# Seven products over all feature tiles in a network's second half, and a quarter of a modulation's dots moved into an earlier stage

## The chip, the core and the metric

The kernel runs on one core of one Trainium2 chip. The metric is the device time of one execution in microseconds (us), the median of several runs. Engines are named as the profile names them: TensorE (PE, with its weight loads PEld), VectorE (DVE), ScalarE (ACT), GpSimd (POOL) and SyncE (SP, which only issues DMAs here).

## The reference

A trunk of two layers runs on 640 tokens at once (128 context tokens, 512 latent ones; 1024 features, so 8 feature tiles of 128). Layer 0 mixes tokens by a two-way SSD scan, layer 1 by differential attention. Behind each mixer stands a gated network, which is where most of the change lies:

```python
def conv_ffn(h, up_w, conv_w, conv_b, down_w):
    u = dwconv(h @ up_w, conv_w, conv_b)      # 1024 -> 2 x 2816, width 3 along the tokens
    a, v = jnp.split(u, 2, axis=-1)
    return (jax.nn.silu(a) * v) @ down_w      # 2816 -> 1024
```

Each sub-layer is normalised, modulated by shift, scale and gate, and added to the residual. The modulation of a layer is `silu(c) @ mod_w + mod_b`, 6 x 1024 values for each of two conditioning vectors (context, latent). Layer 1's ("the second modulation") is first needed by the norm in front of the attention.

## The kernel before

Activations lie feature-major, as tiles of 128 features by 640 tokens. Every large product is made of float32 values split in a high and a low half ("h" and "l", whi and wlo): high x high, high x low and low x high, three matmuls for one. Weights come by DMA as `raw` units of up to 128 x 1024, listed in order by `weight_units`. `cast` makes the halves: ScalarE copies the high one, VectorE subtracts for the low one. For units in the set `summed` the low half is made without VectorE: ScalarE writes the negative of the high half, and a DMA that GpSimd issues adds the weights from DRAM to it (line 181). Before, `summed` holds only up-projection weights of layer 1.

**The network** (`ffn`) computes 22 pairs of hidden tiles (a, v). The plain form takes, for each of the two tiles, 8 feature tiles x 3 products x 2 column halves (256 and 384 columns). From pair `S0[l]` on it uses a scheme with seven block products instead of eight: feature tiles are taken in two groups of `ns`, tokens in two halves of 320, and sums of weight blocks and of activation halves (T1 to T4) are multiplied. `pair8` does so in layer 1 with ns = 4, all eight feature tiles, from pair 4 on. `pair7` does so in layer 0 with ns = 2, on four of the eight feature tiles (the other four stay plain), from pair 16 on. `operands` builds the T tiles (VectorE adds and subtractions, ScalarE copies); in layer 0 they lie in the buffers of the modulation's rows. `epilogue` does convolution, silu and product and splits the result into mh and ml. In layer 1 ml too is made by ScalarE and an accumulating DMA.

The pairs are worked in blocks (`SUB`): after each block, one pair ahead, `project_out` multiplies it with the down weights for all 8 output tiles and `gate_add` adds to the residual `xr`. Layer 0 has three blocks, layer 1 five. `project_last` does the last block and starts the next norm (`norm_task`, by token halves A and B); `start_tiles` begins the next product with three output tiles, half A first.

**The second modulation** is computed by VectorE: `mod_rows` on TensorE serves layer 0 only, and `mod_rest` (line 598) loads the 48 rows of 512 KB of layer 1 one at a time into two `mw` buffers and takes two dots a row (line 620). It is a background task: `hook` is called after every few matmuls (six, most often) and lets tasks emit a next piece, each with its own pace. In layer 0 this task is drained before the down-projection of the second block.

The order of each engine's instructions is set when the program is built, by a list scheduler which takes what is ready, the earlier written first. Engines then run in that order. A pool of SBUF tiles that opens on the room of an earlier one waits until all of that one's tiles are released.

Stages in the trace: scan until 422 us, its output projection (`po`) 422 to 559, layer 0's start tiles (`st`) 559 to 582, its network until 1025, attention until 1390, layer 1's network until the end.

Of the kernel before, what the change touches and what calls it, by code (L numbers as in the profile page):

```python
# [18 lines left out]
P = 128  # L19
# [17 lines left out]
SUB = ((0, 8), (8, 15), (15, 22)), ((0, 4), (4, 8), (8, 12), (12, 16), (16, 22))  # L37
MIDS = 9, 6
# [3 lines left out]
NS = 2, 4  # L42
S0 = 16, 4
# [6 lines left out]
class Step:  # L50


    def __init__(self, ctx, tc, a):
        self.ctx, self.tc, self.nc, self.a = ctx, tc, tc.nc, a
        self.tasks = []
        self.ticks = 0
        self.wi = 0
        self.normt = {}
        self.ready = []
        self.px = None  # L60
        self.modtask = None
        self.late = []
        self.down = False
# [265 lines left out]
    def project_last(self, h, ks, g, nextnorm, ks_last=None, parts="AB"):  # L329
# [268 lines left out]
    def mod_rest(self, l, t0, pool):  # L598
# [3 lines left out]
        cb = pool.tile([P, 2, D], F32, tag="cbc", name="cbc", bufs=1)  # L602
        nc.sync.dma_start(cb, a["cbc"])
        for c in range(2):
            sb = self.pw.tile([P, 1024], F32, tag="raw", name="csil", bufs=RAW)
            self.act(sb, cb[:, c, :], AF.Tanh, scale=0.5)
            self.stt(cb[:, c, :], sb, 1.0, cb[:, c, :], ALU.add, ALU.mult)
            nc.vector.tensor_scalar(cb[:, c, :], cb[:, c, :], 0.5, None, ALU.mult)
        yield 4
        for t in range(t0 - 1, 48):  # L610
            if t < 47:
                nxt = pool.tile([P, 1024], F32, tag="mw", name="mw", bufs=2)
# [6 lines left out]
            for c in range(2):  # L619
                nc.vector.tensor_tensor_reduce(w if c else junk, w, cb[:, c, :], 1.0, 0.0, ALU.mult, ALU.add,  # L620
                                               self.mod[l][:, t, c:c + 1])
                yield 2 if self.down else 7
# [17 lines left out]
    def ffn(self, l, h, nextnorm, pool):  # L640
# [16 lines left out]
        def epilogue(p, ua, uv):  # L657
# [6 lines left out]
            hi = self.slot("mh", f"mh{p}", F32R, bufs=MIDS[l], pool=pool)  # L664
            lo = self.slot("ml", f"ml{p}", F32R, bufs=MIDS[l], pool=pool)
            self.act(hi, cv, AF.Copy)
            if l and p < FT - 1:
# [17 lines left out]
        ns = NS[l]  # L685
        cut = lambda t, j: t[:, j * TH:(j + 1) * TH]

        def operands(out):
# [4 lines left out]
            for i in range(ns):  # L693
# [10 lines left out]
                if l:  # L704
                    hi, lo = (pool.tile([P, 3 * TH], F32R, tag=f"T{nm}{i}", name=f"T{nm}{i}", bufs=1) for nm in "hl")
                    x4 = tuple(cut(t, 1) for t in h[i])
                    late.append((x4, cut(t43, 0)))
                    parts = (slice(0, T), t12), (slice(T, T + TH), cut(t43, 1))
                else:
                    if i:  # L710
                        both = pool.tile([P, 2, 3 * TH], F32R, tag="cbc", name=f"T{i}", bufs=1)
                        hi, lo = both[:, 0, :], both[:, 1, :]
                    else:
                        hi, lo = (pool.tile([P, 3 * TH], F32R, tag="mw", name=f"T{nm}{i}", bufs=2) for nm in "hl")
                    t4 = self.slot("f", f"T4_{i}", F32R, bufs=NF)
                    x4 = cut(t4, 0), cut(t4, 1)
                    late.append((x4, cut(t43, 0)))
                    parts = (slice(0, T), t12), (slice(T, T + TH), cut(t43, 1))
# [63 lines left out]
        def pair7(p, B, Ts, rest, _):  # L782


            (B11, _), (B21, B22) = B
            T1, T2, T3, T4 = Ts
            u = self.wi
            self.wi += 3
            self.prefetch(u + 6)
            self.cast(u + 2)  # L790
            wa, ws, wv = (self.wcast[u + j] for j in range(3))
            w, r0 = ns * P, 2 * ns * P
            ua, uv = (self.slot("f", "uraw", bufs=NF) for _ in range(2))
            p5 = self.slot("f", "p5", bufs=NF)[:, :TH]
            ps = self.dense_ps("up")
            X, Y = ps[:, :TH], ps[:, 512:512 + TH]
            block(X, wa, 0, B11, True, True)
            with self.tc.high_priority():
                self.act(ua[:, lft], X, AF.Copy)
            block(Y, wa, w, B21, True, False)  # L800
            ps = self.dense_ps("up")
            V, Z = ps[:, :TH], ps[:, 512:512 + TH]
            block(V, ws, 0, T1, True, True)
            with self.tc.high_priority():
                self.act(p5, V, AF.Copy)
            block(X, ws, w, T2, False, True, True)
            with self.tc.high_priority():
                self.tt(ua[:, rgt], X, p5, ALU.add)
            block(Y, wa, r0, rest[0], False, True)
            self.tt(ua[:, lft], Y, ua[:, lft], ALU.add)  # L810
            block(Z, ws, 3 * w, B22, True, False)
            self.cast(u + 3)
            block(Z, wa, r0, rest[1], False, True)
            self.tt(ua[:, rgt], Z, ua[:, rgt], ALU.add)
            block(X, ws, 2 * w, T3, False, True, True)
            with self.tc.high_priority():
                self.act(uv[:, rgt], X, AF.Copy)
            self.cast(u + 4)
            block(V, wv, r0, rest[1], False, True, True)
            self.tt(uv[:, rgt], V, uv[:, rgt], ALU.add)  # L820
            block(X, wv, w, T4, False, True, True)
            block(X, wv, r0, rest[0], False, True, True)
            with self.tc.high_priority():
                self.act(uv[:, lft], X, AF.Copy)
            epilogue(p, ua, uv)

# [5 lines left out]
        def pair(p, more):  # L832
            if p >= S0[l]:
# [3 lines left out]
                return pair8(p, more) if l else pair7(p, *sevens)  # L837
# [5 lines left out]
        self.deep = 2 if l else 1  # L843
        sevens = []
        self.began = None
        self.seven = self.add(operands(sevens), 1) if l else None
        for s, (k0, k1) in enumerate(SUB[l]):
            self.down = False
            while done < min(k1 + 1, FT):
                pair(done, done + 1 < min(k1 + 1, FT))  # L850
                done += 1
            self.down = True
            if s == 1 and not l:
                self.drain(self.modtask)
                self.seven = self.add(operands(sevens), 4)
            if s == len(SUB[l]) - 1 and self.modtask:
                self.drain(self.modtask)
            if s < len(SUB[l]) - 1:
                self.project_out(mid, range(k0, k1), self.gate(l, 1))
            else:  # L860
                self.project_last(mid, range(k0, k1), self.gate(l, 1), nextnorm, parts="CD" if l else "AB")
# [269 lines left out]
    def ssd(self, h, dtps, nextnorm, pool):  # L1131
# [51 lines left out]
        for i in range(KT):  # L1183
            xi = self.slot("f", f"xr{i}", bufs=NF)
            self.nc.sync.dma_start(xi, self.a["xT"][i])
            self.x.append(xi)
        self.project_out(hy, range(8), self.gate(0, 0))
# [3 lines left out]
        self.modtask = self.add(self.mod_rows(2, pool, 7))  # L1191
        self.project_last(hy, range(8), self.gate(0, 0), nextnorm)

# [238 lines left out]
    def weight_units(self):  # L1432
# [9 lines left out]
        def ffn(l):  # L1442
            done = 0
            out = []
            ns = NS[l]
            m = ns * 4 * P // 1024
            for k0, k1 in SUB[l]:
                while done < min(k1 + 1, FT):
                    seven = done >= S0[l]
                    pl = ("x", "w") if seven and l else (None, None)  # L1450
# [19 lines left out]
    def run(self):  # L1470
        tc, nc, a = self.tc, self.nc, self.a
        self.units = self.weight_units()
        last = [u for u, x in enumerate(self.units) if x[0] is not None and x[0].name == a["w_up"].name][-2 * FT:]
        after = [u for u in last if self.units[u - 1][0] is not None and self.units[u - 1][0].name != a["w_up"].name]
        self.summed = set(last[5:]) - set(after)
# [10 lines left out]
        with tc.tile_pool(name="psd", bufs=3, space=PSUM) as self.psd:  # L1486
            self.stages(tc, hs, norm)
        with (tc.tile_pool(name="psb", bufs=6, space=PSUM, reuse_waits="tile") as self.psb,
              tc.tile_pool(name="ffn1", bufs=1) as pool):
            self.px = pool  # L1490
            self.modtask = None
            self.ffn(1, hs[3], self.final_task, pool)
            for t in reversed(list(self.tasks)):
                self.drain(t)

    def stages(self, tc, hs, norm):

        with tc.tile_pool(name="sconst", bufs=1) as cp:
# [6 lines left out]
        with tc.tile_pool(name="ffn0", bufs=1) as pool:  # L1505
            self.px = pool
            mw = lambda: pool.tile([P, 1024], F32, tag="mw", name="ntm", bufs=2)

# [105 lines left out]
```

## Time and profile before

| | us |
|---|---|
| median of 3 runs | 1846.98 |
| lowest, highest | 1846.07, 1847.43 |
| the profiled execution | 1847.95 |
| its span, first to last instruction | 1846.2 |
| PE busy in the span | 1802.7 |
| DVE busy | 1490.5 |
| ACT busy | 1038.7 |

The granted TensorE clock is 0.994 of full speed. Durations of matmuls overlap, since they are pipelined: the time of a stage is read from where it starts and ends, and divided by the number of matmuls. A group's line gives the engine, the operation, output and inputs by name, the shape and the count, then busy us, mean ns of one, and the idle time in front with what ended it. VectorE's and ScalarE's instructions overlap by some 0.07 us, so the distance of two starts is a little less than a duration.

### The profile page before, as it was taken

What the parts mean: (1) busy time and instruction counts of PE and PEld (TensorE: products, weight loads), DVE (VectorE), ACT (ScalarE), POOL (GpSimd) and SP (SyncE); (2) the same over time, 40 slices, a digit from 0 to 9 for tenths busy, and PEclk for the clock granted to TensorE, in tenths of its full rate; (3) what the DMA queues carried; (4) which work ended last, traced back from release to release, by engine and by line L of the source; (5) the groups of instructions that cost most, each with busy time, mean ns of one, the idle gap of its engine ahead of it and who ended that gap; (6) DMA issues with size and microseconds to landing.
All of it is one profiled execution on the core that took longest, in us unless ns stands there. A gap on an engine that the chain in (4) does not pass through costs nothing.

```text
span 1846.2 us, 33204 instructions
## 1 busy us (share of the span) xinstructions
PE 1802.7 (98%) x13070; PEld 1704.8 (92%) x13070; DVE 1490.5 (81%) x2969; ACT 1038.7 (56%) x1987; POOL 49.2 (3%) x60
## 2 busy tenths in 40 slices
PE   7999999999999999999999999999999999999997
PEld 5899999999989999999999988888899999999996
DVE  5689999999748999987585878777878877768784
ACT  3489686879326441343353556656636554746561
POOL 0000000000000000000000000000000010101110
PEclk9999999999999999999999999999999999999998
DMA  9844343445533556542122211211124445546451
GB/s 337 264 135 138 99 148 105 121 137 179 187 133 104 194 183 214 194 133 78 57 82 91 80 48 60 65 55 38 55 83 110 104 114 141 126 129 154 122 137 58
DMA packets 90051, 230.28 MB, mean 125 GB/s; under 512 B 10428, under 2 KB 17192, under 8 KB 89768
## 3 DMA queue, kind: packets, MB, share of 16 engines
q1 hardware_dynamic: 81256, 207.13, 34.8%
q0 software_dynamic: 8064, 20.52, 6.6%
q8 instruction: 102, 1.67, 0.4%
q10 hardware_dynamic: 576, 0.52, 0.1%
q14 instruction: 53, 0.43, 0.1%
HBM read 215.29 MB, written 5.96 MB: 120 GB/s over the span
## 4 chain that ended last, share of the span: by engine, by line
PE 86%; DVE 6%; ACT 3%; DMA 3%; issue 2%; SPq 0%; POOL 0%; DVEq 0%; POOLq 0%; ACTq 0%
PE up L110 27%; PE po L110 25%; PE z L110 6%; PE x L110 5%; PE st L110 5%; PE yp L110 3%; PE bc L110 3%; PE q L110 2%; PE k L110 1%; PE modrow L110 1%; PE sl L110 1%; ACT whi L101 1%; PE ov L110 1%; PE v L110 1%; ACT e L101 1%
## 5 line engine op out<-in xcount | busy, mean ns | idle before, releaser
L101 ACT ACTIVATE whi<-raw 128x1024 fp32r<-128x1024 f32 (+3 forms) x243 | 227.8, 939 | 277.3 <-PE po L110 167.4
L107 DVE TENSOR_TENSOR wlo<-raw,whi 128x1024 fp32r<-128x1024 f32 (+3 forms) x207 | 227.0, 1097 | 43.0 <-ACT whi L101 37.5
L104 DVE SCALAR_TENSOR_TENSOR xr<-po,mod,xr 128x256 f32<-128x256 f32 (+2 forms) x279 | 107.8, 432 | 108.9 <-PE po L110 108.8
L110 PE MATMUL po<-mh,whi 128*128 128x256 f32 (+1 forms) x704 | 166.9, 310 | 0.0
L110 PE MATMUL po<-ml,whi 128*128 128x256 f32 (+1 forms) x704 | 166.6, 309 | 0.0
L110 PE MATMUL po<-mh,wlo 128*128 128x256 f32 (+1 forms) x704 | 166.3, 309 | 0.0
L110 PE MATMUL up<-h01l,whi 128*128 128x256 f32 (+1 forms) x596 | 146.2, 308 | 0.0
L110 PE MATMUL up<-h01h,whi 128*128 128x256 f32 (+1 forms) x596 | 146.1, 310 | 0.1
L110 PE MATMUL up<-h01h,wlo 128*128 128x256 f32 (+1 forms) x596 | 145.6, 308 | 0.0
L110 PEld LDWEIGHTS po<-mh,whi 128*128 128x128 f32 x704 | 128.0, 188 | 0.7 <-ACT mh L101 0.5
L110 PEld LDWEIGHTS po<-ml,whi 128*128 128x128 f32 x704 | 128.2, 188 | 0.2 <-DVE ml L107 0.2
L110 PEld LDWEIGHTS po<-mh,wlo 128*128 128x128 f32 x704 | 128.2, 188 | 0.0
L110 PEld LDWEIGHTS up<-h01h,whi 128*128 128x128 f32 x596 | 108.9, 188 | 1.5 <-ACT uraw L101 1.1
L110 PEld LDWEIGHTS up<-h01l,whi 128*128 128x128 f32 x596 | 109.1, 188 | 0.0
L110 PEld LDWEIGHTS up<-h01h,wlo 128*128 128x128 f32 x596 | 109.0, 188 | 0.0
L110 PE MATMUL up<-h11h,whi 128*128 128x320 f32 (+1 forms) x368 | 107.3, 309 | 0.0
L110 PE MATMUL up<-h11l,whi 128*128 128x320 f32 (+1 forms) x368 | 107.2, 309 | 0.0
L110 PE MATMUL up<-h11h,wlo 128*128 128x320 f32 (+1 forms) x368 | 107.1, 309 | 0.0
L104 DVE SCALAR_TENSOR_TENSOR cv<-uraw,fcw,cv 128x511 f32<-128x511 f32 (+1 forms) x176 | 85.3, 545 | 14.8 <-ACT cv L101 14.8
L104 DVE SCALAR_TENSOR_TENSOR ca<-uraw,fcw,ca 128x127 f32<-128x127 f32 (+1 forms) x176 | 86.7, 545 | 8.8 <-ACT ca L101 7.5
L101 ACT ACTIVATE mh<-cv 128x640 fp32r<-128x640 f32 x44 | 32.5, 738 | 88.8 <-DVE cv L107 88.8
L101 ACT ACTIVATE whi<-s 128x512 fp32r<-128x512 f32 (+1 forms) x96 | 52.8, 571 | 52.2 <-DVE s L107 22.7
(531 smaller groups left out, 5074.4 us busy)
## 6 DMA issues: line engine op xcount, KB each, us to landing
raw<-in_w_up SPq DMA_DIRECT2D x88, 512.0 KB, 3.4
mw<-in_modT SPq DMA_DIRECT2D x48, 512.0 KB, 3.8
raw<-in_w_in SPq DMA_DIRECT2D x40, 512.0 KB, 5.5
rb<-rowd SPq DMA_DIRECT2D x40, 512.0 KB, 5.4
raw<-in_w_qkv SPq DMA_DIRECT2D x24, 512.0 KB, 3.3
mr<-in_mod SPq DMA_DIRECT2D x44, 256.0 KB, 5.2
wlo<-in_w_up POOLq DMA_DIRECT2D x17, 512.0 KB, 5.2
mp<-in_modp SPq DMA_DIRECT2D x32, 256.0 KB, 5.4
```

Of the source, the lines that this page charges most:

```text
L101: return self.nc.scalar.activation(out, in_, func, **k)
L104: return self.nc.vector.scalar_tensor_tensor(out, in0, s, in1, op0, op1)
L107: return self.nc.vector.tensor_tensor(out, a, b, op)
L110: return self.nc.tensor.matmul(out, lhsT, rhs, start=start, stop=stop, skip_group_check=more)
```

## The change

- Layer 0's network uses the form of layer 1 (`pair8`, ns = 4) from pair 10 on; `pair7` goes. It has layer 1's five blocks, and 6 buffers of mh and ml instead of 9. The T tiles get a pool of their own (`sums`), which in layer 0 opens before pair 8, on the room of the modulation's rows: the row task is drained there, and the pool of its rows closed. The operands are built from there on.
- PSUM of layer 0's network is six single banks, as in layer 1, instead of three tiles of two banks.
- Low halves by ScalarE and an accumulating DMA now also for layer 0: its up weights except the first five units and the first of each block, ml except that of the last pair, and the units of the scan's output projection from the fourth on. Weights are cast two units ahead there and in layer 0's network, not one.
- Rows 0 to 11 of the second modulation (`EARLY` = 12 of 48) are done in `project_last` of the scan's output projection, one dot each 3 hooks, in tiles of the scan's `rb` tag (3 buffers: two hold the conditioning, one is left for rows). Rows 12 to 47 follow in layer 0's network, one dot each 4 hooks. Conditioning is loaded and put through its silu in both places.

The core of the diff:

```diff
-SUB = ((0, 8), (8, 15), (15, 22)), ((0, 4), (4, 8), (8, 12), (12, 16), (16, 22))
-MIDS = 9, 6
+SUB = (0, 4), (4, 8), (8, 12), (12, 16), (16, 22)
+MIDS = 6
-NS = 2, 4
-S0 = 16, 4
+NS = 4
+S0 = 10, 4
+EARLY = 12
...
-    def mod_rest(self, l, t0, pool):
+    def mod_rest(self, l, t0, t1, cb, alloc, every):
-        cb = pool.tile([P, 2, D], F32, tag="cbc", name="cbc", bufs=1)
-        nc.sync.dma_start(cb, a["cbc"])
         for c in range(2):
+            nc.sync.dma_start(cb[c], a["cbc"][:, c, :])
...
-        for t in range(t0 - 1, 48):
-            if t < 47:
-                nxt = pool.tile([P, 1024], F32, tag="mw", name="mw", bufs=2)
+        for t in range(t0 - 1, t1):
+            if t < t1 - 1:
+                nxt = alloc()
                 nc.sync.dma_start(nxt, a["modT"][t + 1])
...
-                yield 2 if self.down else 7
+                yield every
...
-            if l and p < FT - 1:
+            if p < FT - 1:
                 self.act(lo, cv, AF.Copy, scale=-1.0)
                 nc.gpsimd.dma_start(lo, cv, accum_op=ALU.add)
...
-        for s, (k0, k1) in enumerate(SUB[l]):
...
+        with ExitStack() as ctx:
+            for s, (k0, k1) in enumerate(SUB):
+                while done < min(k1 + 1, FT):
+                    if done == max(S0[l] - 2, 0) if not l else done == 0:
+                        if modpool:
+                            self.drain(self.modtask)
+                            self.modtask = None
+                            modpool.close()
+                        tp = ctx.enter_context(self.tc.tile_pool(name=f"sums{l}", bufs=1))
+                        self.seven = self.add(operands(sevens, tp), 1)
+                    pair(done, done + 1 < min(k1 + 1, FT))
+                    done += 1
...
+        self.deep = 2
         self.project_out(hy, range(8), self.gate(0, 0))
...
+        row = lambda name: pool.tile([P, 1024], F32, tag="rb", name=name, bufs=3)
+        cb = [row("cb0"), row("cb1")]
+        early = self.add(self.mod_rest(1, 0, EARLY, cb, lambda: row("mw"), 3), 1)
         self.project_last(hy, range(8), self.gate(0, 0), nextnorm)
+        self.drain(early)
...
+        self.summed = (set(up) - set(up[:5]) - set(up[half:half + 5]) - after) | set(so[3:])
...
+        with psb() as self.psb, tc.tile_pool(name="ffn0", bufs=1) as pool:
+            self.px = pool
+            modpool = ExitStack()
+            mp = modpool.enter_context(tc.tile_pool(name="mod", bufs=1))
+            mw = lambda: mp.tile([P, 1024], F32, tag="mw", name="mw", bufs=2)
+            cb = [mp.tile([P, 1024], F32, tag="cb", name="cb", bufs=2) for _ in range(2)]
+            self.late = [mw, mw, lambda: self.slot("f", "ntl", bufs=NF)]
+            self.modtask = self.add(self.mod_rest(1, EARLY, 48, cb, mw, 4), 48)
+            self.ffn(0, hs[1], norm(1, 0, hs[2]), pool, modpool)
```

More of the change, by code (lines that the diff above doesn't have):

```diff
@@ L62, in __init__ @@
         self.late = []
-        self.down = False
         self.wraw, self.wcast = {}, {}
@@ L703, in operands @@
                 yield 2
[L704 to L718, printed above, removed]
+                hi, lo = (tp.tile([P, 3 * TH], F32R, tag=f"T{nm}{i}", name=f"T{nm}{i}", bufs=1) for nm in "hl")
+                x4 = tuple(cut(t, 1) for t in h[i])
+                late.append((x4, cut(t43, 0)))
+                parts = (slice(0, T), t12), (slice(T, T + TH), cut(t43, 1))
                 for o, x in parts:
@@ L780, in pair8 @@
             epilogue(p, ua, uv)
[L782 to L825, printed above, removed]
         def finish_operands():
@@ L836, in pair @@
                     finish_operands()
-                return pair8(p, more) if l else pair7(p, *sevens)
+                return pair8(p, more)
             ua = copy_out(self.next_tile(h, "up"))
@@ L842, in ffn @@
         done = 0
-        self.deep = 2 if l else 1
+        self.deep = 2
         sevens = []
         self.began = None
-        self.seven = self.add(operands(sevens), 1) if l else None
-        for s, (k0, k1) in enumerate(SUB[l]):
[L848 to L861, printed above, removed]
+        with ExitStack() as ctx:
[4 more added lines that the diff above has]
+                            self.drain(self.modtask)
+                            self.modtask = None
+                            modpool.close()
[3 more added lines that the diff above has]
+                    done += 1
+                if s < len(SUB) - 1:
+                    self.project_out(mid, range(k0, k1), self.gate(l, 1))
+                else:
+                    self.project_last(mid, range(k0, k1), self.gate(l, 1), nextnorm, parts="CD" if l else "AB")
     def ssd_consts(self, pool):
@@ L1472, in run @@
         self.units = self.weight_units()
-        last = [u for u, x in enumerate(self.units) if x[0] is not None and x[0].name == a["w_up"].name][-2 * FT:]
-        after = [u for u in last if self.units[u - 1][0] is not None and self.units[u - 1][0].name != a["w_up"].name]
-        self.summed = set(last[5:]) - set(after)
+        name = lambda u: self.units[u][0] is not None and self.units[u][0].name
+        up = [u for u in range(len(self.units)) if name(u) == a["w_up"].name]
+        after = {u for u in up if name(u - 1) and name(u - 1) != a["w_up"].name}
+        so = [u for u in range(len(self.units)) if name(u) == a["w_so"].name]
+        half = len(up) // 2
+        self.summed = (set(up) - set(up[:5]) - set(up[half:half + 5]) - after) | set(so[3:])
         self.x = []
@@ L1485, in run @@
         hs = [[] for _ in range(4)]
[L1486 to L1498, printed above, removed]
+        psd = lambda: tc.tile_pool(name="psd", bufs=3, space=PSUM, reuse_waits="tile")
+        psb = lambda: tc.tile_pool(name="psb", bufs=6, space=PSUM, reuse_waits="tile")
+        with psd() as self.psd, tc.tile_pool(name="sconst", bufs=1) as cp:
             with tc.tile_pool(name="first", bufs=1) as pool, tc.manual_schedule():
```

39 lines of the change are left out of this document (21 added, 18 removed).

## The prediction

> **What bounds the kernel now.** I read the page's busy shares first, then the chain of work that ended last in order of time, because it shows the stage and which engine it runs on. From the page and that chain (start us, us, what):
>
> ```profile
> span 1846.2 us, 33204 instructions
> ...
> PE 1802.7 (98%) x13070; PEld 1704.8 (92%) x13070; DVE 1490.5 (81%) x2969; ACT 1038.7 (56%) x1987; POOL 49.2 (3%) x60
> ```
>
> ```profile
> 582.75 105.61 PE up L110 x720
> 688.36 56.30 PE po L110 x384
> 744.66 98.63 PE up L110 x672
> 843.30 49.80 PE po L110 x336
> 893.10 42.34 PE up L110 x284
> 935.48 11.72 PE up L110 x78
> 948.99 13.17 PE up L110 x88
> 962.30 11.64 PE up L110 x78
> 973.94 40.50 PE po L110 x281
> ...
> 1464.06 28.00 PE po L110 x192
> 1492.06 49.26 PE up L110 x336
> ```
>
> TensorE is busy 98% of the span, and in the first network (582 to 1014) the chain is TensorE, product after product: fewer matmuls are a gain, and any wait of TensorE is a loss. VectorE looks free on average (81%). It isn't in this stage, as the table by stage says (us, PE, PEld, DVE, ACT, POOL, clock, DMA share, GB/s):
>
> ```profile
> 465.00:560.00 95.00, 95.00 (x699) 87.08 (x697) 59.65 (x120) 33.68 (x52) 0.00 (x0) 1.00 0.44 148
> ...
> 582.00:745.00 163.00, 163.00 (x1113) 163.00 (x1112) 162.17 (x280) 65.75 (x80) 0.00 (x0) 1.00 0.59 193
> 582.00:702.00 120.00, 120.00 (x818) 120.00 (x817) 119.52 (x204) 58.79 (x73) 0.00 (x0) 1.00 0.55 180
> ```
>
> VectorE works 162.2 of 163 us there, without holding TensorE up: the modulation's dots fill whatever is left, and they may be late until pair 15. The change takes that freedom away.
>
> **The change, part by part.**
>
> *Matmuls.* A plain pair of hidden tiles has 2 x 8 x 3 x 2 = 96 matmuls, pair7 has 90, pair8 has 7 x 4 x 3 = 84. Layer 0 had 16 plain and 6 pair7 (2076), and gets 10 plain and 12 pair8 (1968): 108 fewer. One is issued every 105.61 / 720 = 0.1467 us, and pair8's in layer 1 every 49.26 / 336 = 0.1466 us. That is 108 x 0.1467 = **15.8 us**. The six pair7 took 893.10 to 973.94 = 80.84 us for 540 matmuls, worth 79.2, so 1.6 us of waits at the ends of those pairs go too, since pair8 in layer 1 shows none over 49.26 us. Gain: **17.4 us**. Down-projection matmuls stay the same in number, and five blocks instead of three cost TensorE nothing: 192 in 28.00 us is 0.1458 each.
>
> *VectorE's prices.* Timeline, and groups by shape (busy, mean ns):
>
> ```profile
> 582.27 1.94 DVE L104 SCALAR_TENSOR_TENSOR ca<-uraw,fcw,ca 128x511 f32<-128x511 f32 x4 [0.76 <-ACT ca L101]
> 584.13 1.93 DVE L104 SCALAR_TENSOR_TENSOR cv<-uraw,fcw,cv 128x511 f32<-128x511 f32 x4
> 585.98 1.22 DVE L107 TENSOR_TENSOR wlo<-raw,whi 128x1024 fp32r<-128x1024 f32 x1
> 587.12 0.82 DVE L107 TENSOR_TENSOR cv<-ca,cv 128x640 f32<-128x640 f32 x1
> 587.85 2.35 DVE L104 SCALAR_TENSOR_TENSOR cbc<-csil,cbc 128x1024 f32<-128x1024 f32 x2
> 590.12 0.81 DVE L107 TENSOR_TENSOR ml<-cv,mh 128x640 fp32r<-128x640 f32 x1
> 590.86 1.28 DVE L608 TENSOR_SCALAR cbc<-cbc 128x1024 f32<-128x1024 f32 x2
> ...
> 697.30 1.13 DVE L104 SCALAR_TENSOR_TENSOR xr<-po,mod,xr 128x256 f32<-128x256 f32 x3
> 698.35 1.21 DVE L107 TENSOR_TENSOR wlo<-raw,whi 128x1024 fp32r<-128x1024 f32 x1
> ```
>
> ```profile
> L620 DVE CUSTOM_DVE_ANT_0 mw<-mw,cbc 128x1024 f32<-128x1024 f32 x48 | 58.6, 1221 | 0.8
> ...
> L107 DVE TENSOR_TENSOR wlo<-raw,whi 128x512 fp32r<-128x512 f32 x28 | 19.2, 684 | 0.8 <-ACT whi L101 0.6
> ```
>
> From one start to the next, a pair's epilogue costs 1.86 + 1.85 + 0.74 = 4.45 us without ml, a residual add of an output tile 1.05, a 1024-wide low half 1.14, a 512-wide one about 0.6 (0.684 less the overlap); a modulation row is two dots, 2 x 1.22 = 2.44.
>
> *Deadline in the first network.* All 36 remaining rows are now drained ahead of pair 8, because the sums' tiles take their room. TensorE reaches it at 582.75 + 13 tiles x 7.04 (5 pairs less 3 ready tiles, then 3 pairs) + 28.0 = 702, the next down-projection at 716, pair 10's first product with summed operands at 760. VectorE's work in front of that, from 582: 36 x 2.44 = 87.8; nine epilogues 40.1; 16 residual adds and 16 low halves of the down weights 26.4; the silu of the conditioning again 3.6; two low halves 2.3; operands 4 x (2 x 0.74 + 4 x 0.4 + 1.1) = 16.7; pair 10's first sums 2.4. Together 179.3, and 178 us are there. The 0.4 and 1.1 are scaled by width from the 640-wide 0.74. So VectorE fits with nothing to spare, only since the up weights' low halves and ml leave it for ScalarE and accumulating DMAs. ScalarE hides its part, 58.8 of 120 us busy before and some 13 low halves and eight ml more, 20 us, by these prices of layer 1:
>
> ```profile
> L101 ACT ACTIVATE wlo<-raw 128x1024 fp32r<-128x1024 f32 x13 | 13.6, 1046 | 0.0
> ...
> L101 ACT ACTIVATE ml<-cv 128x640 fp32r<-128x640 f32 x17 | 12.3, 722 | 0.0
> ```
>
>
> *The DMA engines.* Queues of layer 1, where the accumulating kind runs (packets, MB, share of 16 engines), its issues (KB, us to landing), then the plain queue from 465 to 560, the rows' landing, and the load of the conditioning on SP's queue:
>
> ```profile
> q0 software_dynamic: 6743, 16.82, 31.3%
> q1 hardware_dynamic: 9375, 26.76, 24.9%
> ...
> wlo<-in_w_up POOLq DMA_DIRECT2D x13, 512.0 KB, 5.2
> ```
>
> ```profile
> q1 hardware_dynamic: 5826, 13.95, 43.5%
> ```
>
> ```profile
> DMA to landing us min/median/max: 3.1/3.8/4.5
> ```
>
> ```profile
> 578.02 0.33 SPq L603 DMA_DIRECT2D cbc<-in_cbc  x1
> ```
>
> Over those 321 us an accumulating MB occupies 0.313 x 321 / 16.82 = 5.97 us of all engines, a plain one 2.99: 3.13 and 1.57 us for 512 KB. From 578, when the conditioning is loaded, until the rows are in: 36 rows 56, up weights 16 x 1.57 = 25, down weights 16 x 0.78 = 13, the conditioning 3, 13 accumulated weights 41, nine ml of 320 KB 18: 156 us, full until **734** at the least. Copying sums into their tiles takes 4 x 1.1 = 4.4 us on VectorE and some on ScalarE, say 7, so rows may end at 753. I take 3 us of lateness at pair 10 (nothing at a full rate, 12 if the rows go at 80% of it: 578 + 156 / 0.8 = 773, with part of 20 us caught up during the waits).
>
> The Trainium skill bears on this: "DMA: Bandwidth & Descriptors", section "Issuing engines are not separate DMA queues", says that transfers started by different engines share the same 16 DMA engines. By that rule accumulates and rows add up as I have summed them; if instead the two kinds ran side by side, rows would need only their own 97 us and the 3 us would be nothing. The rows cannot decide it: no window before has both kinds near full.
>
> *The early quarter.* Rows 0 to 11 run in project_last of the scan on three "rb" slots, two of which hold the conditioning: one slot is left, so each row loads, is used, and only then the next loads. The slots come free with the last decay; the network's start (chain and timeline):
>
> ```profile
> 461.44 0.39 ACT L101 ACTIVATE m<-rb,Ctok 128x128 f32<-128x128 f32 x1
> ...
> 559.33 1.06 PE st L110 x9
> ```
>
> ```profile
> 561.04 1.22 DVE L107 TENSOR_TENSOR wlo<-raw,whi 128x1024 fp32r<-128x1024 f32 x1
> ```
>
> A row alone takes 3.8 to land + 2.44 + about 0.4 of issue = 6.6 us. The last slot is free at 461.8, a load lands at 466, the silu takes 3.6 of VectorE and waits its turn in the scan's tail: I let the first row start at 474, and the twelfth ends at 474 + 12 x 6.6 = 553. But DMA in 465 to 560 adds 10 accumulates 31 and 14 loads 22 to 0.435 x 95 = 41: 94 of 95 us. Landing at 5 instead of 3.8 gives 7.8 a row and 568. ffn0's pool opens on the scan pool's room, so its first weight slot ("x", the third start tile) waits for the last row; that cast takes ScalarE 1.05 and VectorE 1.14, and TensorE wants it at 562. So rows may end at 559.5, and every us behind it stops TensorE. I take an end at 563: **4 us**, between 0 (553) and 8.5 (568). Twelve rows also put 29 us on VectorE in 95 us of which 59.7 are busy, less ten low halves (11.4); they fit, but 1.2 us dots stand between the steps of both norms: **1.5 us**, between 0 and two rows, 5.
>
> *What stands behind the new waits.* A dot whose row hasn't landed holds VectorE, and residual adds and low halves of down weights queue behind it; TensorE has three output tiles of PSUM, 3 x 3.5 = 10.5 us, before it notices. A row's load that waits for its slot holds SP's queue, and weights behind it come later; four raw buffers of 7 us each cover that. ml and weights share POOL's queue: 56 issues now, about 70 more, each 0.87 us by layer 1's
>
> ```profile
> L181 POOL DMA_DIRECT2D wlo<-in_w_up x30 | 26.2, 875 | 182.5 <-ACT wlo L101 130.9 <-DVE xr L104 31.8 <-PE up L110 19.8
> ```
>
> which idles 182 us of 321 in front of these. I cost all three at nothing; if that cover is gone, it is rival 2 or 3.
>
> *Nothing:* the first matmul operand's PSUM pool (same six banks), two more low halves in advance in the scan, and layer 1's pool for its sums: same work there. Six buffers of mh and ml instead of nine hold a block of four and the pair ahead, as in layer 1.
>
> **The sum.** -17.4 + 3 + 4 + 1.5 = -8.9 us on the profiled execution, 1847.95 (span 1846.2 and 1.75 around it). That run lies 0.97 above the median 1846.98, so 1847.95 - 8.9 - 0.97 = **1838.1**.
>
> **Rivals.**
> 1. *All hidden.* Rows alone need 553 and VectorE needs 179 of 178: nothing late. 1846.98 - 17.4 = 1829.6; with the 2 us that any start costs, to 1833. For it: TensorE has no wait from 1464 on with the same pairs in layer 1. Against: there no rows run beside them.
> 2. *The operands are late.* Rows go at 80% DMA rate and the sums are 12 us late, with the 4 and 1.5 in front: 1846.98 - 17.4 + 17.5 = 1847.1. For it: 179 against 178 and 156 of 156.
> 3. *Slower: the early rows hold the pool.* The price is 1 us per us behind 559.5. With 17.4 gained and 3.7 for 0.2%, it decides when the twelfth row ends at 580.6, or 8.9 us a row. At 9.5 a row (landing 6.7, as in a full queue) it ends at 588: 28.5 late, 1846.98 - 17.4 + 28.5 = 1858; at 8.9, 1851. For it: 94 of 95 us of DMA and a single slot. Against: layer 1's accumulates land in 5.2 us, and its plain weights without delay, at a share of 0.57.
>
> **How the numbers follow.** Forecast (8 us of waits, 1834 to 1843): 0.45. Rival 1: 0.25. Rival 2 (1843 to 1851): 0.15. Rival 3: 0.15. A measurement of this kernel tells 0.2% (3.7 us) from no change, so faster is below 1843.3: 0.70; within: 0.15; slower, above 1850.7: 0.15. The range runs from rival 1 without any loss, 1829, to the foot of rival 3, 1852.
>
> **What would show it.** Right: 1968 up matmuls of layer 0; twelve pairs of 84 at 12.3 us; a DMA share near 0.9 from 480 to 740; a hole of TensorE of a few us at the first start tiles (released by the weight cast behind the last early dot), and one at pair 10 (released by the copy of the sums). Wrong: no hole at the start though the last early dot ends past 560 (then the pool isn't the gate), DMA share below 0.75 while rows are waited for, or holes elsewhere, as in front of residual adds queued behind dots whose row hasn't landed.

## The result and the profile after

The changed kernel takes 1931.81 us (median of 4, 1931.10 to 1934.04) beside 1847.20 for the kernel before on the same chip: **ratio 1.0457, 95% interval 1.0439 to 1.0475**. 1838.1 was forecast. Times are medians; one run of the experiment e6 was slow (6137.51 us) and is left out of its 1856.91, while with it the median is 1858.02, the figure that later expectations use. From the page of the changed kernel:

```profile
span 1930.7 us, 33559 instructions
...
PE 1800.4 (93%) x12962; PEld 1697.8 (88%) x12962; DVE 1503.7 (78%) x3046; ACT 1112.6 (58%) x2136; POOL 109.3 (6%) x129
...
q0 software_dynamic: 18000, 49.42, 14.8%
```

The 108 matmuls are gone (13070 to 12962) and TensorE's busy time fell by 2.3 us, but the span grew by 84.5: the loss is waiting. Where TensorE waits, from 440 to 860 (engine, what, released by: us, times, longest):

```profile
PE st L110 <- ACT whi L101: 56.0, 1, 56.0
PE po L110 <- DMA ml<-cv: 5.5, 2, 4.3
PE po L110 <- ACT uraw L101: 5.5, 1, 5.5
PE ms L110 <- ACT sq L101: 4.5, 2, 3.5
PE po L110 <- DMA wlo<-in_w_so: 4.2, 1, 4.2
```

One wait of 56 us stands out. The chain of work in order of time tells what it is made of, and where the network is in step again:

```profile
542.02 7.74 DMA wlo<-in_w_so
...
633.45 3.21 DMA mw<-in_modT
636.67 1.23 DVE junk L620
637.94 1.22 DVE mw L620
639.21 1.06 ACT whi L101
640.32 8.86 PE st L110 x48
...
847.04 51.02 PE up L110 x348
...
926.22 49.26 PE up L110 x336
```

Load, two dots, load, two dots, and behind the last dot of the early quarter the weight cast of the third start tile. That is the gate that the prediction's third rival named, but it opens at 639, not at 553 to 588. The table by stage (us, PE, PEld, DVE, ACT, POOL, clock, DMA share, GB/s):

```profile
560.00:583.00 23.00, 18.52 (x135) 17.06 (x135) 18.95 (x42) 8.38 (x14) 0.00 (x0) 0.85 0.34 115
583.00:640.00 57.00, 1.35 (x12) 1.15 (x11) 32.03 (x65) 4.90 (x11) 0.00 (x0) 0.55 0.24 83
...
780.00:847.00 67.00, 50.79 (x297) 48.39 (x295) 61.30 (x126) 26.01 (x42) 4.37 (x5) 0.85 0.46 137
847.00:1064.00 217.00, 217.00 (x1485) 217.00 (x1484) 166.01 (x317) 136.16 (x228) 28.74 (x33) 1.00 0.59 141
```

From 847 to 1064 TensorE has no wait at all: the new blocks run as forecast (a pair 49.26 us / 4 = 12.3). Nearly all is lost ahead of them, most of it in two places: the hole of 583 to 640, and 780 to 847, where TensorE works 50.8 of 67 us beside a VectorE that works 61.3. The start tiles also begin 15.8 us later than before (575.12 against 559.33).

Why the rows are so late, the timeline at the norm shows:

```profile
569.37 0.37 PE L110 MATMUL ms<-nsq,cst 128*32 128x96 f32 x8
...
569.81 1.22 DVE L620 CUSTOM_DVE_ANT_0 junk<-mw,cb 128x1024 bf16<-128x1024 f32 x1
```

The first dot starts when the last read of nsq is done. The dots' scrap tile `junk` uses the tag "sq", which has one buffer, and `norm_begin` takes the same tag for the norm's sum at the top of `project_last`. So no early dot can run until that sum has been read for the last time. Twelve rows at 5.8 us each then run from 569.8 to 639.1, in full view.

In the network, VectorE waits for rows as well, from 655 to 850:

```profile
DVE junk L620 <- DMA mw<-in_modT: 21.7, 9, 5.4
```

### The profile page after: what moved, and what is told of

Same layout as the page of the kernel before. It is cut to its first block, busy times and chain, and to the rows that moved or that the text cites. A ratio compares the mean times of both kernels' runs of the same rounds, so it can differ in the third digit from the quotient of the medians.

```text
span 1930.7 us, 33559 instructions
## 1 busy us (share of the span) xinstructions
PE 1800.4 (93%) x12962; PEld 1697.8 (88%) x12962; DVE 1503.7 (78%) x3046; ACT 1112.6 (58%) x2136; POOL 109.3 (6%) x129
## 4 chain that ended last, share of the span: by engine, by line
PE 73%; DVE 14%; DMA 7%; ACT 4%; issue 2%; SPq 0%; DVEq 0%; ACTq 0%
PE po L110 20%; PE up L110 20%; PE z L110 6%; PE x L110 5%; PE st L110 4%; DMA mw<-in_modT 4%; PE bc L110 3%; PE yp L110 3%; DVE mw L620 2%; PE q L110 2%; DVE junk L620 2%; PE k L110 1%; PE v L110 1%; ACT whi L101 1%; PE sl L110 1%
## 5 line engine op out<-in xcount | busy, mean ns | idle before, releaser
L101 ACT ACTIVATE whi<-raw 128x1024 fp32r<-128x1024 f32 (+2 forms) x259 | 227.3, 879 | 279.6 <-PE po L110 125.6
L107 DVE TENSOR_TENSOR wlo<-raw,whi 128x1024 fp32r<-128x1024 f32 (+2 forms) x175 | 172.6, 987 | 26.2 <-ACT whi L101 25.5
L110 PE MATMUL up<-h01l,whi 128*128 128x256 f32 (+1 forms) x464 | 121.8, 310 | 0.0
L110 PE MATMUL up<-h01h,wlo 128*128 128x256 f32 (+1 forms) x464 | 121.8, 310 | 0.0
L181 POOL DMA_DIRECT2D wlo<-in_w_up x70 | 60.9, 870 | 940.2 <-DVE rs_y L218 418.2
L101 ACT ACTIVATE whi<-s 128x512 fp32r<-128x512 f32 x120 | 73.8, 625 | 69.7 <-DVE s L107 34.4
L110 PE MATMUL up<-Tl,whi 128*128 128x320 f32 x360 | 111.2, 309 | 0.0
L110 PE MATMUL up<-Th,whi 128*128 128x320 f32 x360 | 111.0, 308 | 0.0
L110 PE MATMUL up<-Th,wlo 128*128 128x320 f32 x360 | 111.0, 308 | 0.0
L107 DVE TENSOR_TENSOR wlo<-s,whi 128x512 fp32r<-128x512 f32 x120 | 80.6, 685 | 32.9 <-ACT whi L101 32.4
```

What stands on the lines that cost most here:

```text
L101: return self.nc.scalar.activation(out, in_, func, **k)
L107: return self.nc.vector.tensor_tensor(out, a, b, op)
L110: return self.nc.tensor.matmul(out, lhsT, rhs, start=start, stop=stop, skip_group_check=more)
L181: self.nc.gpsimd.dma_start(lo[:, c], self.units[u][0][:, c], accum_op=ALU.add)
```

## The experiments

All ratios are to the kernel before, run beside them. The expectations name theories by letters. **A**: the scrap tile holds the early quarter back. **B**: the rows' deadline ahead of pair 10 is the loss in the network. **C**: the traffic is, the accumulating transfers beside the rows. D to H are said where they come up.

### Undoing parts of the change

**e1_own_junk**: the scrap goes to the scan pool's tag "xw", which is free by then.

```diff
-            junk = self.slot("sq", "junk", BF16, cols=1024, bufs=1)
+            junk = out() if out else self.slot("sq", "junk", BF16, cols=1024, bufs=1)
...
+                                       lambda: pool.tile([P, 1024], BF16, tag="xw", name="junk", bufs=2)), 1)
```

> The early dots write their scrap into a slot of the scan's xw tag instead of the single sq buffer; nothing else changes. Theory A (the single buffer, held by the norm's sum of squares until 569.5, keeps the early dots back, and the pool gate then stops TensorE): the first dot moves from 569.8 to about 505, the twelve rows at 5.75 us end near 574, the start tiles' stage shrinks from 82 us to 25 to 35, and the time falls by 45 to 60, to 1872 to 1887. Theory C (the accumulating DMAs fill the DMA engines and the rows are late whatever slot they have): the dots begin early but need 8 us a row or more, end behind 600, and the time stays above 1900.

1893.08 us, ratio 1.0240 (1.0218 to 1.0261): **38.7 us less from one buffer**. The wait for the cast shrinks from 56.0:

```profile
PE po L110 <- DMA wlo<-in_w_so: 7.6, 2, 4.6
PE st L110 <- ACT whi L101: 7.1, 1, 7.1
```

The first and the last early dot in e1, and the end of the conditioning's silu in the change, which every early dot needs:

```profile
506.81 1.21 DVE L620 CUSTOM_DVE_ANT_0 junk<-mw,cb 128x1024 bf16<-128x1024 f32 x1
...
598.27 1.22 DVE L620 CUSTOM_DVE_ANT_0 mw<-mw,cb 128x1024 f32<-128x1024 f32 x1
```

```profile
503.38 1.28 DVE L608 TENSOR_SCALAR cb<-cb 128x1024 f32<-128x1024 f32 x2
```

A is shown for this part, but it isn't the whole: 45 to 60 us were expected. The first dot comes when the silu is done, and a row then takes 7.7 us (506.8 to 599.5 for twelve), where A had 5.75 and C 8 or more. The dots now run through the norm, so the start tiles begin at 584.2, later than the change's 575.1. Still some 45 us over before.

**e2_no_early** (EARLY = 0, all 48 rows in the network, blocks from pair 10), **e3_no_early_16** (the same, blocks from pair 16), **e4_no_early_16_so** (e3, and the scan projection's low halves by VectorE again):

```diff
-EARLY = 12
+EARLY = 0
...
-S0 = 10, 4
+S0 = 16, 4
...
-        self.summed = (set(up) - set(up[:5]) - set(up[half:half + 5]) - after) | set(so[3:])
+        self.summed = (set(up) - set(up[:5]) - set(up[half:half + 5]) - after)
```

> No early rows: all 48 rows run in layer 0's network and are drained ahead of pair 8. Theory A: the start tiles' stage is back at 23 to 25 us and the norm ahead of it loses nothing, -64 us. Theory B (rows drained ahead of pair 8 are more than VectorE and the DMA engines can do by then): twelve more rows cost 2.44 us of VectorE each and up to 5 with their loads, +29 to +60 in the network. Together 1897 to 1927. If the rows in the network cost nothing (B wrong), 1868.

> No early rows, and seven products only from pair 16 on, so the rows are drained ahead of pair 14: 2040 matmuls of layer 0's up-projection, 36 fewer than before the change (5.3 us, and 1.6 of pair7's waits). Theory B: the network has no hole, and what is left over is the 10 us that the accumulated output-projection weights cost ahead of the start tiles: 1847 - 7 + 10 = 1850. Theory C for the network (accumulating DMAs, not the deadline, hold TensorE there): most of its 29 us stays, 1870 or more.

> As the one before, and the low halves of the scan's output projection are made by VectorE again, as before the change. The theory that the last accumulated unit (issued 542.0, landed 549.8) and the full DMA queue ahead of it cost 10 us: 10 us below the run before, about 1840, and the start tiles begin at 559 to 560. If that wait is only moved: the same time as the run before.

1904.99 (1.0309, 1.0282 to 1.0335), 1891.13 (1.0217, 1.0192 to 1.0242) and 1877.91 (1.0158, 1.0143 to 1.0174). In e2 the hole at the start is gone, and a new one is in the down-projection:

```profile
PE po L110 <- DVE wlo L107: 26.3, 2, 24.4
```

In e2 the start tiles begin at 571.2, and their last matmuls at 593.6 instead of e1's 617.6: the early quarter still cost e1 24 us. In e3 the wait of 26.3 is gone, but not the loss: 1850 was expected if B were all, and 1870 or more by C. e3 is 13.9 us faster than e2 in spite of 72 more matmuls, so the deadline has a price, but B alone fell. From e3 to e4, 13.2 us come from the scan projection, 9.6 of them already where the start tiles begin (572.4 and 562.8): its accumulating transfers were costed at nothing but DMA time. In e4, which has no early rows and a deadline six pairs later, VectorE waits for rows longer than anything else, and TensorE for ml:

```profile
DVE junk L620 <- DMA mw<-in_modT: 35.1, 15, 6.5
```

```profile
PE po L110 <- DMA ml<-cv: 13.5, 3, 5.6
```

### Why e4 still loses 30 us

Theory D: a dot whose row is late blocks VectorE, and what stands behind it is late for TensorE. E: mid's own accumulation is the late one. F: the blocks are slow by themselves; G: VectorE has too much work. Four ways to take one suspect away, each from e4 (e8 reads its 96 dots from two rows, so it leaves layer 1's modulation out):

```diff
e5 (and the up weights of layer 0 out of self.summed), e7
-            if p < FT - 1:
+            if l and p < FT - 1:
e6
+            while t0 + len(nxt) < min(max(t, t0) + AHEAD, t1):
+                nxt.append(alloc())
+                nc.sync.dma_start(nxt[-1], a["modT"][t0 + len(nxt) - 1])
...
-            mw = lambda: mp.tile([P, 1024], F32, tag="mw", name="mw", bufs=2)
+            mw = lambda: mp.tile([P, 1024], F32, tag="mw", name="mw", bufs=AHEAD)
e8
+                if t < t0 + 1:
+                    nxt = alloc()
+                    nc.sync.dma_start(nxt, a["modT"][t + 1])
```

> As e4 (no early quarter, second network's blocks from pair 16, scan projection's low parts by VectorE), and besides no accumulating transfer at all in layer 0: the low parts of the up weights and of mid in the first network are made by VectorE, as before. Theory D (VectorE blocks in order on dots whose row is late, because the accumulating transfers fill the 16 engines; the idle time it gives TensorE then lowers the clock): the waits for rows fall from 35 us to under 10, about 34 us come back less some 3 of VectorE's added work, 1841 to 1850. Theory E (the latency of mid's own accumulation in front of the down-projection) gives the same here. Rival F (the blocks of one network in another layer, with their own banks, are slow by themselves): no change, 1870 to 1880. Rival G (VectorE's added work of about 40 us makes it the bound): slower, 1885 or more.

> As e4, but the rows of the second modulation are loaded four ahead into five buffers instead of one ahead into two; nothing else moves. Theory D in its first half (VectorE waits because a row is asked for one row ahead): the waits for rows fall from 35 us to under 10 and most of the 34 us comes back, 1845 to 1855. If the 16 engines are the limit and not the time ahead: waits stay above 20 us and the time within 8 us of e4, 1870 to 1880. Theory E: no change.

> As e4, but the low part of mid in layer 0 is made by VectorE instead of by an accumulating transfer; the up weights' low parts stay with the transfers. Theory E (mid's accumulation ends late in front of the down-projection): the 13.5 us of po waiting for ml and what the clock loses behind them go, 1853 to 1863. Theory D: the waits for rows remain over 20 us, and the gain is under 10, 1868 to 1878.

> As e4, but only the first two rows of the second modulation are loaded and all dots read those two tiles (the modulation of layer 1 is left out, its numbers are meaningless): VectorE has the same 96 dots and never waits for a row, and 24 MB less pass through the queue. Theory D: nearly all of the 34 us comes back, 1841 to 1850. Theory E: no change beyond what an emptier queue gives mid's accumulation, 1865 or more. Rival G (VectorE's work, not its waits): no change.

e5: 1856.34 (1.0042, 1.0027 to 1.0057). e6: 1856.91 (1.0050, 1.0031 to 1.0069). e7: 1874.44 (1.0144, 1.0121 to 1.0168). e8: 1851.79 (1.0023, 1.0011 to 1.0034). VectorE's waits for rows, in e5 and then in e6:

```profile
DVE junk L620 <- DMA mw<-in_modT: 0.2, 1, 0.2
```

```profile
DVE junk L622 <- DMA mw<-in_modT: 8.0, 5, 2.7
```

An emptier queue, an earlier request and no load at all give 21 to 26 us back, with VectorE's 96 dots in place each time. D is shown, though it was expected to give some 34 and e5, e6 and e8 all came out above their ranges. They lie 4 to 9 us above before, and 9 to 14 when the 5.3 us of the 36 matmuls saved are counted: that is the most that F and G can hold here. In e8 the waits of TensorE from 540 to 1060 are 8.2 us, 3.9 of them in the norms (`ms` for `sq`), where the kernel before has none in that window. E fell: in e7 TensorE waits 0.9 us for ml instead of 13.5, and the time changes by 3.5 us.

e6 is the telling one, since its queue is no emptier (a DMA share of 0.99 from 650 to 700, and 0.82 in e4). For this window, first its DMA queues (packets, MB, share) and issues (KB, us to landing), then the stage (clock, DMA share and GB/s last):

```profile
q1 hardware_dynamic: 3118, 10.33, 57.5%
q0 software_dynamic: 1141, 4.00, 41.0%
...
mw<-in_modT SPq DMA_DIRECT2D x14, 512.0 KB, 14.3
wlo<-in_w_up POOLq DMA_DIRECT2D x7, 512.0 KB, 9.6
```

```profile
650.00:700.00 50.00, 50.00 (x344) 50.00 (x343) 45.54 (x92) 23.79 (x32) 6.97 (x8) 1.00 0.99 288
```

The 16 engines are full, a row takes 14.3 us to land, and TensorE doesn't stop: with four rows asked for ahead the landing time is covered. These rows also stand behind each other: in e4, with one ahead, the median landing in the same window is 3.5 us. The limit was the request, one row ahead, not the rate.

### The deadline by itself

With loads ahead, the blocks are moved back to earlier pairs. **e9_rows_ahead_10** and **e11_rows_ahead_12** are e6 with `S0` = 10 and 12; **e10_no_sums0_12** has 12 and e5's edits; **e12_early8** is the change with its own scrap tile, 8 early rows, loads ahead and the scan projection as before.

> As e6_rows_ahead (no early quarter, rows of the second modulation loaded four ahead, scan projection's low parts by VectorE), but the second network's blocks begin at pair 10 as in the change. The matmuls of six pairs fall to eight tiles: 108 matmuls at 0.1467 us, 15.8 us less than e6. If the deadline costs nothing: 1842. The rows' dots ended at 778 in e6 and must here be done ahead of pair 8, at about 745: 33 us of dots then stand in one block in front of VectorE's other work, so that 15 to 30 of it shows and eats the gain: 1855 to 1872, which I take as likelier.

> Rows loaded four ahead, no accumulating transfer in layer 0 (as e5), blocks from pair 12: 72 matmuls at 0.1467 us, 10.6 less than e5's 1856. If VectorE, which then makes all the low parts, is done with the rows by pair 10 (at about 800): 1846. If it is the bound: 1852 to 1865.

> As e6_rows_ahead, blocks from pair 12: 72 fewer matmuls at 0.1467 us, 10.6 less than e6's 1858. The rows ended at 778 in e6 and are needed by about 800, so the deadline costs nothing: 1847. If the deadline costs (theory of the deadline after all): above 1855.

> The change as made with three things mended and nothing else: the early dots' scrap goes to a buffer of its own (as e1) and only 8 rows are early, so that they end by 553 instead of 569 to 639; the scan projection's low parts are made by VectorE; the rows in the network are loaded four ahead. If the three causes are the whole loss, the forecast's matmul gain of 17.4 remains, less 5 to 8 for the rows in the network that end at about 760 against pair 8's start at 745: 1835 to 1845. If a fourth cause of size is left (the accumulating transfers of the network itself): 1850 or more.

1876.20 (1.0141, 1.0126 to 1.0157), 1877.54 (1.0147, 1.0132 to 1.0162), 1857.56 (1.0040, 1.0025 to 1.0055) and 1869.72 (1.0100, 1.0079 to 1.0121). All four came out too slow: e9 and e10 above the dearer of their ranges (1872 and 1865 at most), e11 and e12 where a cost was to show (above 1855 and 1850), while 1847 and 1835 to 1845 were the values without one. The deadline does cost, 35 us at pair 10 (e9 against e6: 19.3 slower with 15.8 of matmuls saved) and 11 at pair 12 (e11). Without accumulating transfers it costs 32 at pair 12 (e10 against e5: 21.2 slower with 10.6 saved), where VectorE makes the low halves too and TensorE waits for one:

```profile
PE up L111 <- DVE wlo L108: 20.6, 2, 20.0
```

TensorE's timeline in e9, then VectorE's dots in that hole (busy of 33 us, count, clock, DMA share, GB/s):

```profile
764.05 0.90 PE L111 MATMUL po<-mh,wlo 128*128 128x256 f32 x2 [31.04 <-DVE wlo L108]
```

```profile
731.00:764.00 33.00, 24.05 (x42) 0.50 0.30 100
```

24 of 33 us are dots, and what waits behind them is a low half of a *down-projection* weight. Theory H: the dots drained at pair 8 stand in VectorE's order ahead of the down-projection that comes next, not only of pair 10. To tell work from blocks, **e13_36_rows** and **e14_24_rows** are e9 with fewer dots in full (the other rows' dots read 8 columns, so part of layer 1's modulation is left out), and **e15_early4_13** is the whole computation with 4 early rows and the blocks from pair 13:

```diff
e13, e14
+            n = 1024 if t < ROWS else 8
...
e15 (from e12)
-EARLY = 8
+EARLY = 4
-S0 = 10, 4
+S0 = 13, 4
```

> As e9_rows_ahead_10 (no early quarter, rows four ahead, blocks from pair 10), but only 36 of the 48 rows are loaded and their dots made in full; of the last 12 the dots read 8 columns, so a quarter of the modulation of layer 1 is left out. It is the change's network with an early quarter that costs nothing. By the prediction's step (VectorE 179 us of work in 178 us, 3 us of lateness): 29 us of dots less in front of the deadline, 1842 + 3 = 1845. If VectorE's queue in front of pair 10 is later than that sum says (theory H): the hole of 31 us in e9 shrinks by the 29 us of dots less what the clock takes, 1848 to 1856 remains.

> The same with 24 rows in full, the dots of the other 24 over 8 columns: 59 us of dots less than e9 in front of pair 10, no shortage of VectorE left. Both theories then expect 1842 (e6's 1858 less 15.8 of matmuls) if the deadline and the rows are all that is wrong, and also less than e13 by what the prediction left out. If 1850 or more remains, it isn't VectorE's work that makes blocks from pair 10 late but the blocks or the sums themselves.

> Whole computation. As e12_early8, but 4 rows early (done by 535, ahead of the norm) and blocks from pair 13: VectorE has 44 rows in the network and some 45 us more than at pair 10. If VectorE's work in front of the deadline is what costs, no hole is left there: e8's 1851.8 (no row waited for) less three pairs of matmuls, 54 at 0.1467 us, 7.9: 1844. If a hole of e11's size (10 us) remains: 1854.

e13: 1850.44 (1.0008, 0.9999 to 1.0017). e14: 1834.26 (0.9920, 0.9903 to 0.9936). **e15: 1840.76 (0.9955, 0.9940 to 0.9970), faster than both kernels**, 0.45% than the one before. e13 lies in H's range (1848 to 1856), e14 8 us below what was expected of it. The chain's start of pair 9 in e9, e13 and e14, which is 847.04 in the change:

```profile
787.57 51.01 PE up L111 x348
```

```profile
763.97 51.01 PE up L112 x348
```

```profile
748.59 51.02 PE up L112 x348
```

From there on all four run alike (51 us for the same 348 matmuls). So the blocks and the sums are innocent, which settles F, and the number of dots ahead of pair 8 sets the time: 12 rows are 29.3 us of dots and move pair 9 by 23.6 (e9 to e13), and by 15.4 where the queue has partly caught up (e13 to e14). With 36 rows, the change's own number, TensorE still stops three times:

```profile
729.28 0.40 PE L112 MATMUL po<-mh,whi 128*128 128x256 f32 x1 [2.69 <-ACT uraw L103]
736.66 0.90 PE L112 MATMUL po<-mh,wlo 128*128 128x256 f32 x2 [6.38 <-DVE wlo L109]
745.09 0.66 PE L112 MATMUL po<-mh,whi 128*128 128x384 f32 x1 [2.97 <-DVE xr L106]
```

All three are in the second down-projection, released by a copy that waits for VectorE, a low half and a residual add. The last full dot ends at 727; what VectorE works through in front of the last two is mostly the sums and a late epilogue. In e15 the deadline lies three pairs later, and TensorE is busy 99.57 of 100 us there:

```profile
700.00:800.00 100.00, 99.57 (x679) 99.30 (x678) 86.46 (x171) 47.95 (x74) 10.49 (x12) 1.00 0.69 188
```

## Why the prediction was wrong

It was wrong in sign. Rival 3, at 0.15, had the direction and the gate, but put the lateness on slow rows, and it came mostly from the start. Against e14, which has no shortage left but makes only 24 rows in full, the change loses 97.5 us. The start tiles' first matmuls and last (ns min/median/max, first and last start), in the change and in e14, put it in three places:

```profile
L110 PE MATMUL st<-h01h,whi x48: 278/334/583, 575.1 to 656.8; 128*128 128x256 f32 x24, 128*128 128x384 f32 x24
```

```profile
L112 PE MATMUL st<-h01h,whi x48: 276/334/386, 563.1 to 585.5; 128*128 128x256 f32 x24, 128*128 128x384 f32 x24
```

They begin 12.0 us later, take 81.7 us instead of 22.4 (59.3 more), and from their end to pair 9 it is 190.2 (to 847.04) instead of 163.1 (to 748.59), 27.1 more.

- **Matmuls: right.** Pairs take 12.3 us, and in e14, whose clock is before's to 0.001, TensorE is busy 15.8 us less than before (1802.7), which is what the 108 matmuls were worth. Before's span of 1846.2 less 17.4, plus 3.8 for start tiles that begin later in e14 (563.1 against 559.33), is 1832.6 beside e14's 1834.4. Why they begin later is open: in e4 to e14 without early rows they begin between 560.1 and 563.1, and the diff also gives the scan's PSUM pool the argument `reuse_waits="tile"`, which no run undoes. (The 2 us that rival 1 allowed for "any start" stand in no row.) From e14's page:

```profile
PE 1786.9 (97%) x12962; PEld 1688.0 (92%) x12962; DVE 1465.6 (80%) x3055; ACT 1100.6 (60%) x2121; POOL 98.5 (5%) x116
```

- **The early quarter: the step that failed most.** "I let the first row start at 474": it starts at 569.8. I followed the rows' slot ("rb"), and not the dots' other operands: the silu of the conditioning, which ends at 504.7, and the scrap tile, whose single buffer the norm holds until 569.7. The rate of 6.6 us was missed too: 5.8 in the hole, where the DMA share is 0.24, and 7.7 beside the projection (e1), which is the dear case (7.8). The pool as gate was right: TensorE goes on 1.2 us behind the last early dot, in the change (639.2) and in e1 (599.5). Its 4 us are 59 at the start stage. e1 shows the scrap tile's part, 38.7 us back, and e2 the rest.
- **The scan projection's accumulates, counted only as DMA time, cost 13.2 us** (e3 to e4). The clearest piece is the last of them, 7.74 us of landing on the chain, in place of 1.14 of VectorE. A low half needed that soon has no time for ScalarE, POOL's queue and a landing.
- **The disturbed norm, 1.5 us, was too small.** In the change two early dots stand between the norm's last residual adds (569.8 to 573.3), in front of ms, and the start tiles begin 3.9 us later than in e2. Where the dots run through the whole norm it is 13.0 (e1, 584.2 against e2's 571.2), and 8.9 with eight rows (e12, 571.5 against e9's 562.6).
- **The deadline, 3 us, was misplaced.** VectorE's 179 us of work were held against pair 10 at 760. But the rows are drained at pair 8, and the down-projection between needs VectorE from 716 on; three tiles of PSUM cover 10.5 us. e13, with 36 rows and no early quarter, shows 15.4 us where I had 3; of these up to 4 may be the 24 short dots of e13, of 0.16 us each, that the change doesn't have.
- **"A dot whose row hasn't landed holds VectorE ... I cost all three at nothing": wrong.** It cost e4 21 us (e6), and in the change VectorE waited 21.7. About 12 of the 27 us in the network are left for it when e13's 15.4 are taken off. That remainder is argued, since no run has the change's 36 rows with loads one ahead and an early quarter that costs nothing. e2 and e9 are near to it, with 48 rows: e9 is 28.8 us faster by loads ahead and the scan projection together, so by some 15.6 without the latter's 13.2, if the two add up.
- **The DMA sum was somewhat high, and not the limit.** It had the engines full from 578 to 734 at the least; in e13, with 36 rows asked for ahead, the last full dot ends at 727 at a share of 0.80 from 562 on. In the change the share from 480 to 740 is 0.59, where near 0.9 was forecast, and 0.24 in the hole where rows are waited for: the sign that was named for wrong. The rule of the Trainium skill ("DMA: Bandwidth & Descriptors", section "Issuing engines are not separate DMA queues") now has a window in which the two kinds together fill the engines. It agrees: the two queues' shares add up to 98.5% in e6. An accumulated MB took 0.41 x 50 / 4.00 = 5.1 us of all engines there and a plain one 0.575 x 50 / 10.33 = 2.8 (5.97 and 2.99 were used).

## What to carry to other kernels

Filler work that is moved earlier has to be followed through every buffer it touches, the scrap output too: a tag with one buffer that another stage holds is a wait that no queue shows. On an engine that works in order, a deadline lies at the next thing queued behind the filler, not at its consumer, and each filler step needs its data asked for far enough ahead that a busy queue doesn't show. Where work can't be made less, the deadline can be moved: three pairs of blocks given up (7.9 us of matmuls) and four early rows fewer make e15 29 us faster than e12. The two were changed together; 10.8 of the 29 are already there when the start tiles end (595.8 against 585.0), ahead of any block.

## What was unexpected in the hardware

- TensorE's clock falls with its waits and adds to them: 0.55 over the hole in the change, 0.50 in e9's. The 48 matmuls behind the 56 us take 8.86 us, 0.185 each instead of 0.147, some 1.8 us more. In the change TensorE stops at 584.4, and the clock is 1.00 until 589 and 0.50 from 590; in e9 it stops at 727.5, and the clock is 1.00 until 731 and 0.51 behind that. The Trainium skill ("TensorE: Matmul & The Clock Gate", section "What's actually happening") has the clock at half after an idle window of about 3.4 us; both holes agree. Over the whole change the mean clock is 0.971 (0.993 in e14), and TensorE is busy 13.5 us longer than in e14 for the same number of matmuls.
- The landing time of 512 KB rose from 3.2 us (a row alone in the hole) to 14.3 (e6, four asked for ahead, share 0.99) with no TensorE wait: a full queue was no loss there, since the requests were early enough.
